# A two-layer encoder trunk: GpSimd's wide elementwise work on VectorE, and 512-column products with tokens stationary

## The chip, the cores and the metric

One core of a Trainium2 chip. The time is device microseconds of one execution; three unprofiled runs of the kernel before were taken, and one more execution under the profiler.

## The reference

`x` is 256 tokens x 1024, f32. Each of two layers applies three sub-layers, every one as `x = x + weight * rmsnorm(f(rmsnorm(x, g_pre)), g_post)`: a SwiGLU FFN (weight 0.5), a token mixer (weight 1), and a second FFN (weight 0.5).

```python
def swiglu(x, w_gate, w_up, w_down):
    return (jax.nn.silu(x @ w_gate) * (x @ w_up)) @ w_down      # 1024 -> 2816 -> 1024

def token_mixing(h, w_in, ...):
    proj = h @ w_in                                             # q, k, v of groups A, B, C
    o_a = chunk_band_attention(qa, ka, va, rel_bias)            # 6 heads of 64
    o_b = diff_attention(qb, kb, vb, lam, subln_g, lambda_init) # 4 heads, ALiBi
    o_c = stick_breaking_attention(qc, kc, vc)                  # 6 heads
    return jnp.concatenate([o_a, o_b, o_c]) @ w_out

def stick_breaking_attention(q, k, v):                          # per block of queries
    z = q @ k * scale
    log_beta = log_sigmoid(z)
    log_one_minus = where(strict, log_sigmoid(-z), 0.0)
    suffix = cumsum(log_one_minus, reverse=True) - log_one_minus
    a = where(strict, exp(log_beta + suffix), 0.0)
    return a @ v
```

## The kernel before

The six sub-layers are numbered `i` = 0 to 5: FFN, mixer, FFN, FFN, mixer, FFN. `x` stays in SBUF (`xs`), two tiles `t` of 128 tokens. Every f32 operand of a wide product is split into a high part of type fp32r and the rest, and `mm3` (L378 to L381) issues three matmuls: high by high, high by low, low by high.

**Weights** come through one `Stream` (L100 to L161). SyncE loads a chunk of 512 KB into one of four `raw` buffers; ScalarE casts it to `whi` (L142), VectorE subtracts to get `wlo` (L143), each in two pieces. `stream.ahead(n)` cuts the next n pieces, `stream.done(n)` frees the buffers of n used chunks, of which there are nine. Where these calls stand in the program sets where the pieces stand in ScalarE's and VectorE's queues.

**A norm** between sub-layers (class `Norm`, L305 to L375) scales the sub-layer's result, adds it to `xs`, and makes the next sub-layer's input `xg`: ScalarE sums squares by halves of 512 columns, GpSimd multiplies the first half by the gain and VectorE the second (`half_pre`, L355 to L359), VectorE adds the mean (L291), GpSimd takes the power (L286), VectorE and ScalarE scale one half each (L365, L366). PE transposes `xg` (`pt`, L374), and `split_copy` makes `xT`, high and low.

**An FFN** does its first 512 hidden columns with tokens stationary (`tokens_out`, L383): groups of 256 columns, gate and up, two of each, for both t; then `ht = sg * pu` on VectorE (L507), PE transposes it (`pth`, L513). The other 2304 columns go with weights stationary (`cols_pair`, L402: for each weight tile one matmul of 512 columns with the high and low parts of `xT`, L411, and one of 256, L413). `down` (L421) has tokens stationary and 512 columns.

```python
        pairs = [[c, c + 1], [c + 2, c + 3], [c + 4, c + 5], [c + 6, c + 7]]
        def gate(p, t, between=None):
            pg = psum.tile([P, 256], F32, tag="rot", name=f"pg{i}_{p}_{t}")
            tokens_out(pg, pairs[2 * p], t, between)
```

**A mixer** computes the values with tokens stationary in three groups of 384, 384 and 256 columns (L611 to L633), then queries and keys tile by tile (`pp`, `qkT`), while the heads' work is put between those products by a table of slots (`PLAN`): each head is a generator, and each of its steps has a slot number. `make_alibi` (L588) fills 4 x 256 columns on GpSimd (L593), `make_bias` (L642) negates the 128x1536 relative bias on GpSimd (L643; slot 41.05). A pair of stick-breaking heads (`pair_c`, L649 to L718; three pairs) makes the scores `s_c`, softplus `e` on ScalarE and VectorE (L678 to L682), its high part on ScalarE and the rest `l1`, `l0` on GpSimd (L690, L691), the sums `u_c` on PE, `z_c` on VectorE (L703, L704), the exponential on ScalarE (L706) and the products `o_c` on PE (L745). The softplus of pairs 0 and 2 and the bias lie in one tile, `yb`.

```python
            nc.gpsimd.tensor_sub(l1, e[:, 512:], h1.bitcast(F32))
            nc.gpsimd.tensor_sub(l0, e[:, :512], h0.bitcast(F32))
```

The first FFN (i = 0) begins while nothing has arrived yet; a table `START` sets the order of its first pieces, some of them on GpSimd.

Of the kernel before, what the change touches and what calls it, by code (L numbers as in the profile page):

```python
# [9 lines left out]
F32 = mybir.dt.float32  # L10
# [6 lines left out]
P = 128  # L17
# [10 lines left out]
QC, KC, VC = 1920, 2304, 2688  # L28
YA, YB, YC = 0, 384, 640
EPS = 1e-6  # L30
NEG = -1e30
FAR = 1e30

CH = 1152
NRAW = 4
# [44 lines left out]
}  # L80
NSPLIT = 9

# [17 lines left out]
class Stream:  # L100
# [64 lines left out]
def trunk_kernel(  # L165
    ctx: ExitStack,
    tc: tile.TileContext,
    x, f1_pre, f1_gate, f1_up, f1_down, f1_post,
    m_pre, w_in, rel_map, lq1, lk1, lq2, lk2, sub_g, w_out, m_post,
    f2_pre, f2_gate, f2_up, f2_down, f2_post,  # L170
# [55 lines left out]
    def plan_ffn(gate, up, down, l):  # L226
        g = {}
        for key, ap, c0 in (("g", gate, 0), ("u", up, 0), ("g", gate, 1), ("u", up, 1)):
            for h in range(2):
                stream.add(rows(ap, l, 4 * h, 4 * h + 4, c0 * 256, c0 * 256 + 256), 4, 256)  # L230
# [7 lines left out]
    V_CUTS = ((0, 3), (3, 6), (6, 8))  # L238
    QK_TILES = (
# [6 lines left out]
    def plan_mix(l):  # L246
        for c in (VC, VA):
            for k0, k1 in V_CUTS:
                stream.add(rows(w_in, l, k0, k1, c, c + 384), k1 - k0, 384)
        for h in range(2):  # L250
            stream.add(rows(w_in, l, 4 * h, 4 * h + 4, VB, VB + 256), 4, 256)
# [53 lines left out]
    class Norm:  # L305
# [6 lines left out]
        def post(self, banks, weight, slack=lambda k: None, last=None):  # L312
# [15 lines left out]
            for h in range(2):  # L328
                nc.vector.scalar_tensor_tensor(xs[:, t, HALVES[h]], fg[:, HALVES[h]], r[:, 0:1],  # L329
                                               xs[:, t, HALVES[h]], ALU.mult, ALU.add)  # L330
                if last is None:
                    self.half_pre(h)
                else:
                    last(t, h)
# [19 lines left out]

        def half_pre(self, h):  # L355
            t, sl = self.t, HALVES[h]
            mean_square(xs[:, t, sl], self.ss, h, "pre" + self.nm)
            eng = nc.gpsimd if h == 0 else nc.vector
            eng.tensor_mul(self.xg[:, sl], xs[:, t, sl], pre_tiles[self.i][:, sl])  # L359

        def end_pre(self):
            self.r = rstd_of(halves_mean(self.ss, "pre" + self.nm), 1, "pre" + self.nm)

            xg = self.xg
            nc.vector.tensor_scalar(xg[:, :512], xg[:, :512], self.r[:, 0:1], None, ALU.mult)  # L365
            nc.scalar.activation(xg[:, 512:], xg[:, 512:], AF.Copy, scale=self.r[:, 0:1])  # L366
# [27 lines left out]
    def cols_out(ps, c, quarter=lambda q: None):  # L394
# [79 lines left out]
    def ffn(i, turn1):  # L474
# [18 lines left out]

        pairs = [[c, c + 1], [c + 2, c + 3], [c + 4, c + 5], [c + 6, c + 7]]

        def gate(p, t, between=None):
            pg = psum.tile([P, 256], F32, tag="rot", name=f"pg{i}_{p}_{t}")
            tokens_out(pg, pairs[2 * p], t, between)
            sg = work.tile([P, 512], F32, tag="ta", bufs=TA, name=f"sgt{i}_{p}_{t}")
            nc.scalar.activation(sg[:, :256], pg, AF.Silu)  # L500
            return sg

        def up(sg, p, t, between=None):
            pu = psum.tile([P, 256], F32, tag="rot", name=f"pu{i}_{p}_{t}")
            tokens_out(pu, pairs[2 * p + 1], t, between)
            h = work.tile([P, 512], F32, tag="tb", bufs=3, name=f"ht{i}_{p}_{t}")
            nc.vector.tensor_mul(h[:, :256], sg[:, :256], pu)  # L507
            return h

        def token_close(h, p, t):  # L510
            pt = psum.tile([P, 2, P], F32, tag="rot", name=f"pth{i}_{p}_{t}")
            for j in range(2):
                nc.tensor.transpose(pt[:, j, :], h[:, j * P : j * P + P], ident)  # L513
            ts = slice(t * P, t * P + P)
            split_copy(hT_hi(2 * p, 2)[:, :, ts], hT_lo(2 * p, 2)[:, :, ts], pt)

        sg00 = gate(0, 0, (lambda: start(1)) if i == 0 else None)
        if i == 0:
            start(2)
        h00 = up(sg00, 0, 0, (lambda: start(3)) if i == 0 else None)  # L520
        if i == 0:
            start(4)
        else:
            sg10 = gate(1, 0, turn1)
        sg01 = gate(0, 1)
        stream.done(2)
        if i == 0:
            stream.ahead(4)
        h01 = up(sg01, 0, 1)
        stream.done(2)  # L530
        stream.ahead(4)
        if i == 0:
            sg10 = gate(1, 0)
        sg11 = gate(1, 1)
        stream.done(2)
        stream.ahead(4)
        new_h()
        token_close(h00, 0, 0)
        h10 = up(sg10, 1, 0)
        token_close(h01, 0, 1)  # L540
        h11 = up(sg11, 1, 1)
        stream.done(2)
        stream.ahead(4)
        token_close(h10, 1, 0)
        load_pre(i + 1)
        if i % 3 == 0:
            load_lambda(i // 3)
        closing = [(h11, 1, 1)]
        for f in range(4, KF, 2):
# [31 lines left out]
    def mix(i, l, turn1):  # L581
# [27 lines left out]
        c = stream.used  # L609
        vgroups = [(YC, [c, c + 1, c + 2], 384, "acc"), (YA, [c + 3, c + 4, c + 5], 384, "acc"),  # L610
                   (YB, [c + 6, c + 7], 256, "rot")]  # L611

        def values(g, t, between=None):
            y0, chunks, n, tag = vgroups[g]
            pv = psum.tile([P, 512], F32, tag=tag, name=f"pv{l}_{g}_{t}")
            tokens_out(pv[:, :n], chunks, t, between)
            (nc.scalar.copy if g != 1 else nc.vector.tensor_copy)(v[:, t, y0 : y0 + n], pv[:, :n])

        values(0, 0)
        stream.ahead(2)  # L620
        values(1, 0, turn1)
        stream.ahead(2)
        nc.scalar.preload_act_table_set("natural_log_exp_and_others")
        values(0, 1)
        stream.done(3)
        stream.ahead(6)
        values(1, 1)
        stream.done(3)
        stream.ahead(6)
        values(2, 0)  # L630
        values(2, 1)
        stream.done(2)
        stream.ahead(6)  # L633
        qkT = act.tile([P, 16, SEQ], F32, tag="bigh1", name=f"qkT{l}")
# [14 lines left out]
        def pair_c(j):  # L649
# [104 lines left out]
        def head_b(h):  # L754
# [51 lines left out]
        def head_a(h):  # L806
# [164 lines left out]
```

## Time and profile before

| | |
|---|---|
| median of 3 runs | 1038.41 us (1036.89 to 1039.23) |
| the profiled execution: own time / span | 1042.82 us / 1041.1 us |
| PE (TensorE) busy | 1018.3 us, 98% |
| VectorE (DVE) busy | 676.4 us, 65% |
| ScalarE (ACT) busy | 588.8 us, 57% |
| GpSimd (POOL) busy | 89.0 us, 9% |
| TensorE's mean granted clock | 0.986 |
| DMA | 183.16 MB, mean 176 GB/s |

The span runs from the first to the last instruction of the profiled execution; its own time is measured as that of the unprofiled runs is. A granted clock of 1.0 is 2.4 GHz and 0.5 is 1.2 GHz. A matmul's row shows when it starts and a modelled end, so that neighbours overlap; the step from one start to the next is what a matmul takes of the engine.

### The profile page before, as it was taken

The numbers are of one execution on the slowest core, as the hardware profiler recorded it, in microseconds if no ns is written. First come the engines' busy times: TensorE is split into PE (matmuls) and PEld (weight loads), VectorE is DVE, ScalarE is ACT, GpSimd is POOL, SyncE is SP. The second block draws the span as 40 slices with busy tenths as digits, with TensorE's granted clock in tenths as the row PEclk, the third lists the DMA queues.
The fourth block names the chain that finished last, engine by engine and source line by source line (L and its number), as shares of the span: only waits on it lengthen the run. The fifth ranks groups of instructions, "written<-read, shape, count | busy, mean of one in ns | idle before, by whom it ended". The sixth has DMA issues, their size and how long they took to land. (4 is left out here: it accounts for less than half of the span.)

```text
span 1041.1 us, 16033 instructions
## 1 busy us (share of the span) xinstructions
PE 1018.3 (98%) x5940; PEld 888.6 (85%) x5940; DVE 676.4 (65%) x1313; ACT 588.8 (57%) x1265; POOL 89.0 (9%) x105
## 2 busy tenths in 40 slices
PE   8899999999999999999999999999999999999997
PEld 7788888898887988888899888888998789888886
DVE  4576774668666677665566876656776665877642
ACT  5465654567655556654446666545666655756531
POOL 3100000111311100000030000002123020000000
PEclk9999999999899999999999999999998999999999
DMA  8866566566244366656726766664933334865631
GB/s 270 219 204 200 184 211 208 145 203 192 82 122 122 117 210 220 197 189 219 215 73 208 244 195 195 222 198 121 261 107 103 117 97 143 261 190 186 222 120 40
DMA packets 151005, 183.16 MB, mean 176 GB/s; under 512 B 5744, under 2 KB 134896, under 8 KB 150928
## 3 DMA queue, kind: packets, MB, share of 16 engines
q1 hardware_dynamic: 148448, 174.08, 54.2%
q0 software_dynamic: 2192, 7.54, 2.7%
q8 instruction: 46, 0.75, 0.3%
q10 hardware_dynamic: 288, 0.52, 0.1%
q14 instruction: 31, 0.25, 0.1%
HBM read 181.08 MB, written 1.05 MB: 175 GB/s over the span
## 5 line engine op out<-in xcount | busy, mean ns | idle before, releaser
L143 DVE TENSOR_TENSOR wlo<-raw,whi 128x512 fp32r<-128x512 f32 (+1 forms) x625 | 403.2, 700 | 169.2 <-ACT whi L142 168.7
L142 ACT CAST whi<-raw 128x512 fp32r<-128x512 f32 x630 | 350.0, 617 | 120.5 <-PE acc L381 70.8
L411 PE MATMUL pg<-xT,whi 128*128 128x512 f32 x576 | 205.5, 398 | 0.0
L411 PE MATMUL pu<-xT,whi 128*128 128x512 f32 x576 | 203.2, 395 | 0.0
L413 PE MATMUL pg<-xT,wlo 128*128 128x256 f32 x576 | 162.2, 282 | 0.0
L413 PE MATMUL pu<-xT,wlo 128*128 128x256 f32 x576 | 161.5, 280 | 0.0
L379 PE MATMUL acc<-whi,hh 128*128 128x512 f32 x352 | 137.2, 390 | 0.0
L381 PE MATMUL acc<-whi,hl 128*128 128x512 f32 x352 | 137.0, 389 | 0.0
L380 PE MATMUL acc<-wlo,hh 128*128 128x512 f32 x352 | 137.0, 389 | 0.0
L411 PEld LDWEIGHTS pg<-xT,whi 128*128 128x128 f32 x576 | 108.7, 189 | 25.2
L411 PEld LDWEIGHTS pu<-xT,whi 128*128 128x128 f32 x576 | 108.0, 187 | 25.3
L413 PEld LDWEIGHTS pg<-xT,wlo 128*128 128x128 f32 x576 | 109.7, 190 | 0.0
L413 PEld LDWEIGHTS pu<-xT,wlo 128*128 128x128 f32 x576 | 108.8, 189 | 0.0
L379 PE MATMUL pp<-xT,whi 128*128 128x256 f32 x256 | 78.9, 308 | 0.0
L379 PEld LDWEIGHTS acc<-whi,hh 128*128 128x128 f32 x352 | 66.1, 188 | 13.7
L381 PEld LDWEIGHTS acc<-whi,hl 128*128 128x128 f32 x352 | 66.1, 188 | 13.7
L380 PEld LDWEIGHTS acc<-wlo,hh 128*128 128x128 f32 x352 | 66.1, 188 | 13.5
L380 PE MATMUL pp<-xT,whi 128*128 128x256 f32 x256 | 74.4, 291 | 0.0
L381 PE MATMUL pp<-xT,wlo 128*128 128x256 f32 x256 | 74.2, 290 | 0.0
L286 POOL TENSOR_TENSOR r_post<-v_post,mhalf 128x1 f32<-128x1 f32 x12 | 6.6, 552 | 779.5 <-DVE v_post L291 779.5
L379 PEld LDWEIGHTS pp<-xT,whi 128*128 128x128 f32 x256 | 51.0, 199 | 7.7 <-issue 7.2
L418 ACT COPY side_pu<-pu 128x256 f32<-128x256 f32 x72 | 26.1, 368 | 47.9 <-PE pu L413 47.9
(247 smaller groups left out, 1559.0 us busy)
## 6 DMA issues: line engine op xcount, KB each, us to landing
raw<-in_ffn_w_gate_dram SPq DMA_DIRECT2D x88, 512.0 KB, 4.8
raw<-in_ffn_w_up_dram SPq DMA_DIRECT2D x88, 512.0 KB, 4.7
raw<-in_ffn_w_down_dram SPq DMA_DIRECT2D x88, 512.0 KB, 4.4
raw<-in_w_in_dram SPq DMA_DIRECT2D x36, 512.0 KB, 5.6
raw<-in_w_out_dram SPq DMA_DIRECT2D x16, 512.0 KB, 3.5
raw<-in_w_in_dram SPq DMA_DIRECT2D x8, 576.0 KB, 4.5
gpost<-in_ffn_post_g_dram POOLq DMA_DIRECT2D x4, 512.0 KB, 4.6
raw<-in_w_in_dram SPq DMA_DIRECT2D x4, 384.0 KB, 3.5
```

What stands on the lines that cost most here:

```text
L142: self.nc.scalar.copy(self.hi[:, a:b], raw[:, a:b])
L143: (lo or self.nc.vector).tensor_sub(self.lo[:, a:b], raw[:, a:b], self.hi.bitcast(F32)[:, a:b])
L286: nc.gpsimd.tensor_tensor(r[:, :width], v, mhalf[:, :width], ALU.pow)
L379: nc.tensor.matmul(ps, lhsT=ah, rhs=bh, start=first, stop=False)
L380: nc.tensor.matmul(ps, lhsT=ah, rhs=bl, start=False, stop=False)
L381: nc.tensor.matmul(ps, lhsT=al, rhs=bh, start=False, stop=last)
L411: nc.tensor.matmul(ps.rearrange("p a t -> p (a t)"), lhsT=wh[:, k % 4, cs], rhs=xT[:, k].rearrange("p a t c -> p (a t c)"), start=k == 0, ...
L413: nc.tensor.matmul(ps[:, 1, :], lhsT=wl[:, k % 4, cs], rhs=xT[:, k, 0].rearrange("p t c -> p (t c)"), start=False, stop=k == KT - 1)
L418: nc.scalar.copy(side, ps[:, 1, :])
```

## The change

GpSimd's wide elementwise work goes to VectorE: the first half of `xg` in ten norms, the alibi and bias multiplications, and `l1`, `l0` of the six stick-breaking pairs. GpSimd keeps the powers, memsets, iota, its DMA issues, and its pieces of the start. In a norm, both multiplications now stand in `end_pre`, around the mean.

Products with tokens stationary take 512 columns, in chunks of two k-tiles x 512: the FFNs' token stage (i = 2, 3, 5) is gate and up of four chunks each, for both t; the values of a mixer are two groups of 512, from an array `w_val` in which the host puts the value columns of C, B and A side by side. The first FFN keeps its groups of 256. With `last=True` (t = 1) `tokens_out` frees each chunk as soon as it is used and cuts two pieces ahead. A split buffer has 1024 columns instead of 1152, and there are ten instead of nine. PE's program has 5235 rows where it had 5625: 384 matmuls fewer (3 x 96 and 2 x 48), each with its weight load.

```diff
-CH = 1152
+CH = 1024
-NSPLIT = 9
+NSPLIT = 10
...
     def plan_ffn(gate, up, down, l):
+        if not stream.src:
...
+        else:
+            for ap in (gate, up):
+                for q in range(4):
+                    stream.add(rows(ap, l, 2 * q, 2 * q + 2, 0, 512), 2, 512)
...
+        for g in range(2):
+            for q in range(4):
+                stream.add(rows(w_val, l, 2 * q, 2 * q + 2, 512 * g, 512 * g + 512), 2, 512)
...
                 if last is None:
-                    self.half_pre(h)
+                    mean_square(xs[:, t, HALVES[h]], self.ss, h, "pre" + self.nm)
...
         def end_pre(self):
-            self.r = rstd_of(halves_mean(self.ss, "pre" + self.nm), 1, "pre" + self.nm)
+            t, xg, g = self.t, self.xg, pre_tiles[self.i]
+            nc.vector.tensor_mul(xg[:, :512], xs[:, t, :512], g[:, :512])
+            v = halves_mean(self.ss, "pre" + self.nm)
+            nc.vector.tensor_mul(xg[:, 512:], xs[:, t, 512:], g[:, 512:])
+            self.r = rstd_of(v, 1, "pre" + self.nm)
...
-    def tokens_out(ps, chunks, t, between=None):
+    def tokens_out(ps, chunks, t, between=None, last=False):
...
                 k += 1
+            if last:
+                stream.done()
+                stream.ahead(2)
...
+            gates, ups = list(range(c, c + 4)), list(range(c + 4, c + 8))
+            h0 = up(gate(gates, 0), ups, 0, turn1)
+            new_h()
+            sg1 = gate(gates, 1, None, True)
+            token_close(h0, 0, 4, 0)
+            closing = [(up(sg1, ups, 1, None, True), 0, 4, 1)]
...
-                nc.gpsimd.tensor_scalar(out=alibi[:, h, :], in0=dneg, scalar1=slope, scalar2=None, op0=ALU.mult)
+                nc.vector.tensor_scalar(out=alibi[:, h, :], in0=dneg, scalar1=slope, scalar2=None, op0=ALU.mult)
...
+            pv = psum.tile([P, 512], F32, tag="acc", name=f"pv{l}_{g}_{t}")
+            tokens_out(pv, list(range(c + 4 * g, c + 4 * g + 4)), t, between, t == 1)
...
-            nc.gpsimd.tensor_scalar(out=biasA, in0=biasA, scalar1=-1.0, scalar2=None, op0=ALU.mult)
+            nc.vector.tensor_scalar(out=biasA, in0=biasA, scalar1=-1.0, scalar2=None, op0=ALU.mult)
...
-            nc.gpsimd.tensor_sub(l1, e[:, 512:], h1.bitcast(F32))
-            nc.gpsimd.tensor_sub(l0, e[:, :512], h0.bitcast(F32))
+            nc.vector.tensor_sub(l1, e[:, 512:], h1.bitcast(F32))
+            nc.vector.tensor_sub(l0, e[:, :512], h0.bitcast(F32))
```

Lines of the changed kernel are numbered a little differently (the weight subtraction is L144, the bias L642). VectorE's queue around the first stick-breaking pair of layer 0, first as it was (`z_c_0` is the pair's score tile, `o_b` is group B's output, `wlo` a weight piece):

```order
L682 SCALAR_TENSOR_TENSOR yb_2378<-z_c_0_2741,yb_2378 128x768
L785 TENSOR_SCALAR yb_2378<-o_b_2_2791,rib_2_2650 128x64 x2
L143 TENSOR_TENSOR wlo_2804<-raw_2576,whi_2803 128x512 x2
L785 TENSOR_SCALAR yb_2378<-o_b_1_2834,rib_1_2563 128x64 x2
L785 TENSOR_SCALAR yb_2378<-o_b_0_2782,rib_0_2556 128x64 x2
L143 TENSOR_TENSOR wlo_2856<-raw_2611,whi_2855 128x512 x2
L703 TENSOR_TENSOR z_c_0_2741<-z_c_0_2741,u_c_0_2889 128x256
L704 TENSOR_TENSOR z_c_0_2741<-z_c_0_2741,u_c_0_2892 128x512
```

And in the changed kernel, on through the second pair's softplus (L681):

```order
L681 SCALAR_TENSOR_TENSOR yb_2334<-z_c_0_2697,yb_2334 128x768
L784 TENSOR_SCALAR yb_2334<-o_b_2_2747,rib_2_2606 128x64 x2
L144 TENSOR_TENSOR wlo_2760<-raw_2532,whi_2759 128x512
L689 TENSOR_TENSOR hl_c_0_2774<-yb_2334,hl_c_0_2774 128x256
L690 TENSOR_TENSOR l_c_0_2773<-yb_2334,h_c_0_2772 128x512
L144 TENSOR_TENSOR wlo_2760<-raw_2532,whi_2759 128x512
L784 TENSOR_SCALAR yb_2334<-o_b_1_2790,rib_1_2519 128x64 x2
L784 TENSOR_SCALAR yb_2334<-o_b_0_2738,rib_0_2512 128x64 x2
L144 TENSOR_TENSOR wlo_2812<-raw_2567,whi_2811 128x512 x2
L702 TENSOR_TENSOR z_c_0_2697<-z_c_0_2697,u_c_0_2845 128x256
L703 TENSOR_TENSOR z_c_0_2697<-z_c_0_2697,u_c_0_2848 128x512
...
L681 SCALAR_TENSOR_TENSOR e_c_1_2857<-z_c_1_2856,e_c_1_2857 128x768
L642 TENSOR_SCALAR yb_2334<-yb_2334 128x1536
```

The two splits of pair 0 (L689, L690) now stand between two weight pieces ahead of z_c, and the bias negation (L642), which GpSimd had after those splits, stands behind the second pair's softplus.

VectorE's queue at the end of FFN 2's token stage as it was (`ht` the multiplication L507, `hl` the split of its transpose):

```order
L143 TENSOR_TENSOR wlo_3786<-raw_3581,whi_3785 128x512 x2
L303 TENSOR_TENSOR hl_2_3795<-pth_0_0_3797,hh_2_3793 128x2x128
L507 TENSOR_TENSOR ht_1_0_3827<-sgt_1_0_3678,pu_1_0_3802 128x256
L303 TENSOR_TENSOR hl_2_3795<-pth_0_1_3829,hh_2_3793 128x2x128
L507 TENSOR_TENSOR ht_1_1_3859<-sgt_1_1_3775,pu_1_1_3834 128x256
L143 TENSOR_TENSOR wlo_3862<-raw_3740,whi_3861 128x512 x2
L143 TENSOR_TENSOR wlo_3870<-raw_3748,whi_3869 128x512 x2
L303 TENSOR_TENSOR hl_2_3795<-pth_1_0_3877,hh_2_3793 128x2x128
```

And in the changed kernel:

```order
L309 TENSOR_TENSOR hl_2_3611<-pth_0_0_3672,hh_2_3609 128x4x128
L144 TENSOR_TENSOR wlo_3687<-raw_3626,whi_3686 128x512 x2
L144 TENSOR_TENSOR wlo_3701<-raw_3640,whi_3700 128x512 x2
L144 TENSOR_TENSOR wlo_3715<-raw_3654,whi_3714 128x512 x2
L144 TENSOR_TENSOR wlo_3729<-raw_3668,whi_3728 128x512 x2
L514 TENSOR_TENSOR ht_102_1_3736<-sgt_98_1_3670,pu_102_1_3679 128x512
L309 TENSOR_TENSOR hl_2_3611<-pth_0_1_3758,hh_2_3609 128x4x128
```

The pieces of four chunks now stand ahead of the last `ht`, where before they stood behind it.

## Rows read from the trace of the kernel before

**Rows 1.** The page, part 1: busy us (share of the span) of each engine, instructions.

```profile
PE 1018.3 (98%) x5940; PEld 888.6 (85%) x5940; DVE 676.4 (65%) x1313; ACT 588.8 (57%) x1265; POOL 89.0 (9%) x105
```

**Rows 2.** Waits of PE: engine, output, line, releaser: us in total, times, longest.

```profile
PE o_c L745 <- ACT yb L706: 4.2, 2, 2.1
PE pth L513 <- DVE ht L507: 3.9, 1, 3.9
...
PE pt L374 <- DVE xg L365: 1.4, 2, 0.7
...
PE s_b L750 <- ACT qkT L847: 0.6, 1, 0.6
PE pv L381 <- DVE xT L303: 0.6, 2, 0.3
```

**Rows 3.** Timeline, layer 0, first stick-breaking pair: start, us, engine, line, op, xcount [idle before].

```profile
268.92 4.64 DVE L143 TENSOR_TENSOR wlo<-raw,whi 128x512 fp32r<-128x512 f32 x2
...
269.36 4.53 POOL L643 TENSOR_SCALAR yb<-yb 128x1536 f32<-128x1536 f32 x1
...
273.48 0.41 DVE L703 TENSOR_TENSOR z_c<-z_c,u_c 128x256 f32<-128x256 f32 x1
...
274.58 0.84 ACT L706 ACTIVATE yb<-z_c 128x768 f32<-128x768 f32 x1 [5.07 <-DVE z_c L704]
...
275.47 0.98 PE L745 MATMUL o_c<-yb,v 128*64 128x256 f32 x4 [2.10 <-ACT yb L706]
```

**Rows 4.** Windows: us, busy time (instructions) of each engine, granted clock, DMA share, GB/s.

```profile
275.67:285.91 10.24, 10.24 (x42) 8.57 (x40) 5.55 (x13) 8.13 (x14) 2.41 (x2) 0.50 0.21 82
784.26:794.50 10.24, 10.24 (x43) 9.29 (x42) 5.62 (x12) 7.14 (x13) 2.42 (x2) 0.50 0.25 70
336.87:340.29 3.42, 2.70 (x16) 2.06 (x16) 1.39 (x5) 1.94 (x4) 0.54 (x1) 1.00 0.00 0
43.56:46.98 3.42, 3.42 (x13) 2.93 (x12) 2.73 (x5) 1.18 (x3) 0.00 (x0) 0.50 0.80 218
```

**Rows 5.** Timeline of PE: first and last of eleven matmuls, 256, then 512 columns.

```profile
20.92 0.28 PE L379 MATMUL pg<-whi,xT 128*128 128x256 f32 x1
...
22.12 0.28 PE L380 MATMUL pg<-wlo,xT 128*128 128x256 f32 x1
...
500.70 0.39 PE L379 MATMUL acc<-whi,hh 128*128 128x512 f32 x1
...
502.97 0.39 PE L380 MATMUL acc<-wlo,hh 128*128 128x512 f32 x1
```

**Rows 6.** Groups of VectorE by form: busy us, mean ns, idle before.

```profile
L359 DVE TENSOR_TENSOR xg<-xs,gpre 128x512 f32<-128x512 f32 x10 | 16.7, 1667 | 0.3
...
L365 DVE TENSOR_SCALAR xg<-xg,r_pre 128x512 f32<-128x512 f32 x10 | 5.0, 500 | 7.0 <-POOL r_pre L286 7.0
...
L704 DVE TENSOR_TENSOR z_c<-z_c,u_c 128x512 f32<-128x512 f32 x6 | 4.1, 680 | 0.6 <-PE u_c L701 0.6
```

**Rows 7.** Timeline of the first FFN, token stage's close.

```profile
38.84 1.14 ACT L142 CAST whi<-raw 128x512 fp32r<-128x512 f32 x2 [2.95 <-DMA raw<-in_ffn_w_up_dram]
...
39.49 2.73 DVE L143 TENSOR_TENSOR wlo<-raw,whi 128x512 fp32r<-128x512 f32 x4 [3.35 <-ACT whi L142]
...
42.48 0.41 DVE L507 TENSOR_TENSOR ht<-sgt,pu 128x256 f32<-128x256 f32 x1
```

**Rows 8.** Timeline, layer 0, second stick-breaking pair.

```profile
288.58 0.28 PE L694 MATMUL u_c<-hl_c,tri 128*128 128x256 f32 x1
...
290.58 0.85 ACT L706 ACTIVATE e_c<-z_c 128x768 f32<-128x768 f32 x1 [1.00 <-DVE z_c L704]
...
294.55 0.66 PE L745 MATMUL o_c<-e_c,v 128*64 128x256 f32 x4
```

**Rows 9.** Windows of PE, line 411: eleven product pairs, then ten.

```profile
609.75:613.56 3.81, 3.81 (x12) 1.00 0.49 155
876.67:880.21 3.54, 3.54 (x12) 1.00 0.78 249
```

More of the change, by code (lines that the diff above doesn't have):

```diff
@@ L28 @@
 QC, KC, VC = 1920, 2304, 2688
-YA, YB, YC = 0, 384, 640
+VYC, VYB, VYA = 0, 384, 640
 EPS = 1e-6
@@ L154, in get @@
     def get(self, i):
+        while i not in self.parts:
+            at = self.cut, self.piece
+            self.ahead(1)
+            assert at != (self.cut, self.piece), "no buffer for a chunk that is needed"
         return self.parts[i]
@@ L168, in trunk_kernel @@
     x, f1_pre, f1_gate, f1_up, f1_down, f1_post,
-    m_pre, w_in, rel_map, lq1, lk1, lq2, lk2, sub_g, w_out, m_post,
+    m_pre, w_in, w_val, rel_map, lq1, lk1, lq2, lk2, sub_g, w_out, m_post,
     f2_pre, f2_gate, f2_up, f2_down, f2_post,
@@ L226, in plan_ffn @@
     def plan_ffn(gate, up, down, l):
[L227 to L230, printed above, removed]
+        if not stream.src:
+            for ap, c0 in ((gate, 0), (up, 0), (gate, 256), (up, 256)):
+                for h in range(2):
+                    stream.add(rows(ap, l, 4 * h, 4 * h + 4, c0, c0 + 256), 4, 256)
+        else:
+            for ap in (gate, up):
+                for q in range(4):
+                    stream.add(rows(ap, l, 2 * q, 2 * q + 2, 0, 512), 2, 512)
         for f in range(4, KF, 2):
@@ L236, in plan_ffn @@
             stream.add(rows(down, l, k, k + 1, 0, D), 1, D)
-    V_CUTS = ((0, 3), (3, 6), (6, 8))
     QK_TILES = (
@@ L246, in plan_mix @@
     def plan_mix(l):
[L247 to L251, printed above, removed]
+        for g in range(2):
+            for q in range(4):
+                stream.add(rows(w_val, l, 2 * q, 2 * q + 2, 512 * g, 512 * g + 512), 2, 512)
         for c in QK_TILES:
@@ L492, in hT_lo @@
             return tiles(hl, 14, k, n)
[L494 to L500, printed above, removed]
-            return sg
[L503 to L507, printed above, removed]
-            return h
@@ L510, in token_close, with gate @@
-        def token_close(h, p, t):
-            pt = psum.tile([P, 2, P], F32, tag="rot", name=f"pth{i}_{p}_{t}")
-            for j in range(2):
+        def gate(chunks, t, between=None, last=False):
+            n = stream.src[c][2]
+            pg = psum.tile([P, 512], F32, tag="rot", name=f"pg{i}_{chunks[0]}_{t}")[:, :n]
+            tokens_out(pg, chunks, t, between, last)
+            sg = work.tile([P, 512], F32, tag="ta", bufs=TA, name=f"sgt{i}_{chunks[0]}_{t}")[:, :n]
+            nc.scalar.activation(sg, pg, AF.Silu)
+            return sg
@@ new lines, in up, with token_close @@
+        def up(sg, chunks, t, between=None, last=False):
+            n = stream.src[c][2]
+            pu = psum.tile([P, 512], F32, tag="rot", name=f"pu{i}_{chunks[0]}_{t}")[:, :n]
+            tokens_out(pu, chunks, t, between, last)
+            h = work.tile([P, 512], F32, tag="tb", bufs=3, name=f"ht{i}_{chunks[0]}_{t}")[:, :n]
+            nc.vector.tensor_mul(h, sg, pu)
+            return h
+        def token_close(h, k, n, t):
+            pt = psum.tile([P, 4, P], F32, tag="rot", name=f"pth{i}_{k}_{t}")[:, :n, :]
+            for j in range(n):
@@ L513, in token_close @@
                 nc.tensor.transpose(pt[:, j, :], h[:, j * P : j * P + P], ident)
             ts = slice(t * P, t * P + P)
-            split_copy(hT_hi(2 * p, 2)[:, :, ts], hT_lo(2 * p, 2)[:, :, ts], pt)
-        sg00 = gate(0, 0, (lambda: start(1)) if i == 0 else None)
+            split_copy(hT_hi(k, n)[:, :, ts], hT_lo(k, n)[:, :, ts], pt)
         if i == 0:
+            pairs = [[c, c + 1], [c + 2, c + 3], [c + 4, c + 5], [c + 6, c + 7]]
+            sg00 = gate(pairs[0], 0, lambda: start(1))
@@ L519, in ffn @@
             start(2)
-        h00 = up(sg00, 0, 0, (lambda: start(3)) if i == 0 else None)
-        if i == 0:
+            h00 = up(sg00, pairs[1], 0, lambda: start(3))
             start(4)
-        else:
[L524 to L544, printed above, removed]
+            sg01 = gate(pairs[0], 1)
+            stream.done(2)
+            stream.ahead(4)
+            h01 = up(sg01, pairs[1], 1)
+            stream.done(2)
+            stream.ahead(4)
+            sg10 = gate(pairs[2], 0)
@@ new lines, in ffn @@
+            sg11 = gate(pairs[2], 1)
+            stream.done(2)
+            stream.ahead(4)
+            new_h()
+            token_close(h00, 0, 2, 0)
+            h10 = up(sg10, pairs[3], 0)
+            token_close(h01, 0, 2, 1)
+            h11 = up(sg11, pairs[3], 1)
+            stream.done(2)
+            stream.ahead(4)
+            token_close(h10, 2, 2, 0)
+            closing = [(h11, 2, 2, 1)]
+        else:
+            gates, ups = list(range(c, c + 4)), list(range(c + 4, c + 8))
+            h0 = up(gate(gates, 0), ups, 0, turn1)
+            new_h()
+            sg1 = gate(gates, 1, None, True)
+            token_close(h0, 0, 4, 0)
+            closing = [(up(sg1, ups, 1, None, True), 0, 4, 1)]
@@ L547, in ffn @@
             load_lambda(i // 3)
-        closing = [(h11, 1, 1)]
         for f in range(4, KF, 2):
@@ L609, in mix @@
         c = stream.used
-        vgroups = [(YC, [c, c + 1, c + 2], 384, "acc"), (YA, [c + 3, c + 4, c + 5], 384, "acc"),
-                   (YB, [c + 6, c + 7], 256, "rot")]
         def values(g, t, between=None):
[L614 to L617, printed above, removed]
+            pv = psum.tile([P, 512], F32, tag="acc", name=f"pv{l}_{g}_{t}")
+            tokens_out(pv, list(range(c + 4 * g, c + 4 * g + 4)), t, between, t == 1)
+            (nc.vector.tensor_copy if g else nc.scalar.copy)(v[:, t, 512 * g : 512 * g + 512], pv)
         values(0, 0)
@@ L621, in mix @@
         values(1, 0, turn1)
-        stream.ahead(2)
         nc.scalar.preload_act_table_set("natural_log_exp_and_others")
         values(0, 1)
-        stream.done(3)
-        stream.ahead(6)
         values(1, 1)
[L628 to L633, printed above, removed]
+        stream.ahead(4)
         qkT = act.tile([P, 16, SEQ], F32, tag="bigh1", name=f"qkT{l}")
@@ L710, in pair_c @@
             for h in range(2):
-                vs = slice(YC + 64 * (2 * j + h), YC + 64 * (2 * j + h) + 64)
+                vs = slice(VYC + 64 * (2 * j + h), VYC + 64 * (2 * j + h) + 64)
                 columns_out(o, h, v[:, :, vs], e0[:, h, :], e1[:, h, :])
@@ L773, in head_b @@
             yield
-            vs = slice(YB + 64 * h, YB + 64 * h + 64)
+            vs = slice(VYB + 64 * h, VYB + 64 * h + 64)
             pT = turned(f"b{l}_{h}", p0)
@@ L824, in head_a @@
                 pair_out[h // 2] = psum.tile([P, SEQ], F32, tag="rot", name=f"o_{nm}")
-            vs = slice(YA + 64 * h, YA + 64 * h + 64)
+            vs = slice(VYA + 64 * h, VYA + 64 * h + 64)
             columns_out(pair_out[h // 2], h % 2, v[:, :, vs], w[:, 0:2, :], w[:, 2, :])
@@ L938 @@
     "x", "ffn1_pre_g", "ffn1_w_gate", "ffn1_w_up", "ffn1_w_down", "ffn1_post_g",
-    "mix_pre_g", "w_in", "rel_map", "diff_lambda_q1", "diff_lambda_k1", "diff_lambda_q2",
+    "mix_pre_g", "w_in", "w_val", "rel_map", "diff_lambda_q1", "diff_lambda_k1", "diff_lambda_q2",
     "diff_lambda_k2", "diff_subln_g", "w_out", "mix_post_g",
@@ L956 @@
     dist = _np.clip(P + _np.arange(P)[:, None] - _np.arange(SEQ)[None, :], -CLIP, CLIP) + CLIP
-    inputs = dict(inputs, rel_map=rb[:, :, dist].transpose(0, 2, 1, 3))
+    w_in = _np.asarray(inputs["w_in"])
+    w_val = _np.concatenate([w_in[:, :, VC : VC + 384], w_in[:, :, VB : VB + 256], w_in[:, :, VA : VA + 384]], axis=2)
+    inputs = dict(inputs, rel_map=rb[:, :, dist].transpose(0, 2, 1, 3), w_val=w_val)
     arrays, args = {}, []
```

6 lines of the change are left out of this document (removed).

## The prediction, made blind

> **What bounds the kernel now.** I read the page's busy times first. TensorE (PE) is busy 98% of the span and GpSimd (POOL) 9% [rows 1], so taking work off GpSimd is worth nothing by itself: only PE's own work and PE's waits count. The list of PE's waits comes next [rows 2]. The reader is to see that few are left: two of 2.1 us before the output products of a stick-breaking pair (o_c), one in the first FFN, some tenths elsewhere.
>
> The timeline of the first pair in layer 0 shows where the 2.1 us is from [rows 3]. GpSimd's negation of the 128x1536 bias table runs from 269.36 for 4.53 us. Two weight pieces on VectorE (DVE) start at 268.92 and take 4.64 us together, where such subtractions of 512 columns take 0.68 each [rows 6], so 1.4. The subtraction z_c stands behind them, starts at 273.48, the exponential follows at 274.58, and o_c starts at 275.47 after 2.10 us of waiting. The other wait of this name is layer 1's.
>
> The windows show what follows [rows 4]: in the 10.24 us from 275.67, and from 784.26 in layer 1, the granted clock is 0.50, the lower of its two levels (1.2 GHz), though PE is busy throughout. Before that it had stood for most of a 2.1 us wait. In the third window PE was also short of work (2.70 of 3.42 us) and kept 1.00. In the fourth, behind the first FFN's wait of 3.9 us [rows 2], it had 0.50 for 3.42 us. So a stall costs its own length and then, if it is long enough, half of the time at the lower level.
>
> **The change part by part.** Measured against the profiled execution, 1042.8 us (span 1041.1); the median of the runs shown, 1038.4, is 4.4 lower.
>
> *Longer products.* With tokens stationary and 256 columns, a step from one matmul to the next is 120 ns: ten steps in 22.12 - 20.92 = 1.20 us [rows 5]. With 512 columns it is 227 ns: ten in 2.27 us. So doubling the columns saves 13 ns per matmul dropped. An FFN's token stage goes from 192 x 120 = 23.04 us to 96 x 227 = 21.77, -1.27; three FFNs change (i = 2, 3, 5), -3.8. The values have 96 matmuls of 384 columns (halfway, 173 ns) and 48 of 256, 22.40 us, and get 96 x 227 = 21.77: -0.63 per layer. Together **-5.1**. This work is on the path, since PE is never without the next matmul there.
> The Trainium skill (TensorE: Matmul & The Clock Gate, the section "Wait — 56ns, not 53.3ns?") states that a step at the full clock is the columns over 2.4 GHz and about 2.5 ns. By that, 384 fewer matmuls would be worth 384 x 2.5 = 1.0 us, an estimate from the page. The rows above disagree, 120 where that rule has about 109, and the rows decide here.
>
> *The bias negation on VectorE.* The 4.53 us on GpSimd become at most three times a VectorE multiplication by a scalar of 512 columns, 0.50 each [rows 6]: 1.5 us, and the order puts it behind the second pair's softplus (L681), no longer ahead of the first pair's z_c. What was doubled on VectorE falls back from 4.64 to 1.4, 3.3 us less. The two splits l1 and l0 are now VectorE's too, 0.68 and at most 0.68 (its 256 columns are half of that row's), ahead of the same z_c. So z_c comes at least 3.3 - 1.4 = 1.9 us earlier, and up to 2.9 where the splits fill time in which VectorE waited for a cast anyway; PE wanted o_c 2.1 earlier. I take both waits as gone, **-4.2**; at the low end 0.2 each stays.
>
> *The clock.* If the waits go, nothing ahead of the two low windows differs from other stretches of that stage, which have the full clock. Work that took 10.24 us at half speed takes 5.12: **-10.2** for both. Bounds: nothing, if another stall takes over, and 10.2.
>
> *The norm.* Two multiplications of 512 columns that ran at the same time, 1.67 us on VectorE [rows 6], become two in a row on VectorE, 2 x 0.68 = 1.36, with the mean between them, so that GpSimd's power and the second multiplication overlap. From the mixer to the FFN PE waits 0.7 us for the scaled rows, twice [rows 2]. Bounds: 0.3 to 0.7 each; I take 0.5, since the mean also waits for ScalarE's second square sum: **-1.0**. The other norms lie behind PE work that covers them (they show no wait), and cost nothing.
>
> *Values.* PE waits 0.3 us for the second half of xT in each layer [rows 2]; with 512 columns the products on the first half last longer by 12 x (227 - 173) = 0.6: **-0.6**. The alibi multiplications, eight of 256 columns at 0.50 or less, are 2 us per layer on VectorE at the stage's start; there VectorE has idle time, I cost them at nothing, and if that cover goes, they delay weight pieces by up to 2 us. The 0.6 us of s_b [rows 2] I leave as it is.
>
> *New waits.* In the FFNs with the new path the pieces of the next four chunks are issued ahead of the multiplication ht of the last token group. ht must end before PE's closing transposes. The first FFN has such an order today: VectorE's pieces from 39.49 for 2.73 us, behind a cast that waited 2.95 us for a transfer, and ht only at 42.48 [rows 7]; that wait costs 3.9 [rows 2]. Its cause is the start's crowded transfers, here they run steadily. If the pieces find their data, the eight casts and subtractions end about when PE wants ht: 0 to 1 us per FFN, taken as 0.4 x 3 = 1.2. In the second stick-breaking pair PE has 5.97 us from u_c at 288.58 to o_c at 294.55, and its exponential began at 290.58 [rows 8], so it was done 3.1 us early; at the full clock PE arrives there up to 2.1 + 5.1 = 7.2 us earlier; VectorE's chain starts earlier too, but is not itself faster, and the negation and two splits stand in it. I count 0.4 per layer, bounds 0 and 1.5. **+2.0** in all.
>
> Sum: -5.1 - 4.2 - 10.2 - 1.0 - 0.6 + 2.0 = **-19.1**. From the profiled execution that is 1023.7, from the median 1019.3. Part of the 4.4 between them may be time that the low clock cost this execution alone, which the unprofiled runs have less of to win back; I take **1020**.
> One term neither part of the change touches: products with weights stationary advance 346 ns per pair in one FFN (3.81 us for 11) and 354 in another (3.54 for 10) [rows 9]. Which step a stage falls into seems set by its start, and the starts move. With 288 pairs per FFN it is 2.2 us each way, for up to three FFNs; the likeliest case has 1012 to 1027 as its own range.
>
> **The rivals.**
> *A stall moves to the second pair.* For it: PE arrives earlier at the full clock, with a margin I make nearly zero. Against: the exponential was 3 us early and VectorE loses its 4.64 us. A wait of 1.5 us in each layer, and 1.7 (as in the first FFN) to 5.1 us of low clock behind it, gives back 6.4 to 13.2: 1026 to 1033, about **1030**.
> *Slower: the FFN closes.* ht stands behind four chunks' pieces in FFN 2, 3 and 5. If their transfers land some 4 us late, PE stands as in the first FFN: 3.9 us and 1.7 to 5.1 of clock, 5.6 to 9.0 each, 17 to 27 for three. It decides from about 7 us each: below, the other gains pay for it, above, the kernel is slower, up to **1047**. For it: the first FFN's wait. Against: VectorE's load there came from the start; in the later FFNs before, the same stage shows no wait.
> *The longer products return little.* If the 13 ns is not a cost of each matmul but is set by the weight loads of these stages, then 5.1 becomes 1.0 or less, and the result is **1024**. For it, the rule of the page cited above; against, rows 5, where both lengths run beside weight loads.
>
> **How the numbers follow.** Forecast 0.70, second pair 0.20, FFN closes 0.05, short return 0.05. The smallest difference that a measurement of this kernel can tell from none is about 0.2%, 2.1 us. Only the second rival, in its upper half, reaches no change or slower; with something for what I don't see: faster 0.95, same 0.02, slower 0.03. The range goes from 1011 (1019.3 less the 2.0 of new waits and the faster step of rows 9 in two or three FFNs) to 1031, which takes in most of the first rival.
>
> **What would show it.** Right: o_c is gone from PE's waits, PE's clock is 1.00 in both mixers, z_c of the first pair starts some 2 us earlier against the PE instruction that wants it, the token stages of FFN 2, 3 and 5 last 1.3 us less, PE's wait for the scaled rows (pt, from the mixer to the FFN) is 0.2 or less. Wrong: 0.50 in a window behind a pth or a second o_c wait; a step other than 227 ns in the 512-column stages; a wait of PE for weight pieces (wlo, whi), which are behind the added VectorE work.

## The result, and the profile after

The changed kernel takes 1034.3 us (median of 15 executions, 1030.8 to 1037.1), the kernel before beside it 1039.3 (1034.4 to 1047.2): ratio 0.9938, 95% interval 0.9918 to 0.9957. That is 5.0 us less by the medians and 6.4 by the ratio. Forecast were 1020 and a range from 1011 to 1031. The direction was right, at least two thirds of the gain is missing.

The profiled execution took 1034.26 us, 8.6 less than the one shown of before. The page's part 1 of the changed kernel, against [rows 1]:

```profile
PE 1005.8 (97%) x5556; PEld 860.2 (83%) x5556; DVE 672.9 (65%) x1333; ACT 586.6 (57%) x1249; POOL 43.2 (4%) x73
```

PE has 5556 matmuls where it had 5940, the 384 fewer on which the prediction counts (the numbers of program rows named ahead, 5625 and 5235, differ by 390). VectorE, which took over GpSimd's wide work, is busy 3.5 us less than before. PE's waits, against [rows 2] (us in total, times, longest):

```profile
PE pth L520 <- DVE ht L514: 10.9, 4, 2.7
...
PE s_b L749 <- ACT qkT L846: 2.3, 2, 1.7
...
PE pt L377 <- DVE xg L368: 1.0, 2, 0.5
```

The waits for o_c and pv are gone; pth, the transposes that close a token stage, has taken their place, with four waits instead of one (the first FFN's, and 2.74 us in each of FFN 2, 3 and 5). To see where the time went I took, in each trace, the start of each stage's first matmul, and the differences:

| stage (us) | before | changed | difference |
|---|---|---|---|
| up to the first FFN's weights-stationary stage | 43.14 | 44.57 | +1.4 |
| token stages, FFN 2 / 3 / 5 | 24.75 / 24.75 / 24.74 | 23.16 / 23.16 / 23.18 | -4.7 |
| weights stationary, FFN 2 / 3 / 5 | 102.02 / 100.20 / 102.02 | 105.11 / 104.81 / 104.84 | **+10.5** |
| values, layer 0 / 1 | 24.25 / 24.26 | 22.67 / 22.67 | -3.2 |
| queries, keys and heads, layer 0 / 1 | 78.64 / 77.96 | 72.75 / 71.71 | **-12.1** |
| output product and the norm behind it | 32.05 / 32.05 | 31.83 / 31.82 | -0.5 |

These make up the 8.6. The +1.4 of the first row lies in the start: the granted clock is 0.50 there for 6.83 us (10.52 to 17.35) in the changed kernel's profile and for 3.41 us (12.84 to 16.26) in that of before, worth up to 1.7 us by an estimate; a second profile of before, shown below, has 10.24 us of it (8.83 to 19.07), so this difference is not put down to the change. The mixers gained what was hoped; the three FFNs gave 10.5 back, right behind their token stages. The timeline of that place in FFN 2 (start, us, engine, line, operation, xcount, and the idle time before with its releaser):

```profile
351.56 0.60 PE L520 MATMUL pth<-ident,ht 128*128 128x128 f32 x4
351.76 0.60 ACT L506 ACTIVATE sgt<-pg 128x512 f32<-128x512 f32 x1 [2.04 <-PE pg L384]
...
355.90 0.39 PE L384 MATMUL pu<-spare,xT 128*128 128x512 f32 x1
...
356.32 0.59 ACT L308 CAST hh<-pth 128x512 fp32r<-128x512 f32 x1 [3.97 <-PE pu L384]
356.81 4.26 ACT L143 CAST whi<-raw 128x512 fp32r<-128x512 f32 x8
...
357.55 4.90 DVE L144 TENSOR_TENSOR wlo<-raw,whi 128x512 fp32r<-128x512 f32 x8
362.37 0.69 DVE L514 TENSOR_TENSOR ht<-sgt,pu 128x512 f32<-128x512 f32 x1
...
363.20 0.63 PE L520 MATMUL pth<-ident,ht 128*128 128x128 f32 x4 [2.74 <-DVE ht L514]
```

PE transposes the first token half at 351.56, but ScalarE's copy `hh` of it starts only at 356.32, 4.0 us after the silu, released by a PE product. The products up to 355.90 read `spare`: two weight chunks lie in that tile, which `hh` takes next (it has the same tag). So the copy waits for the last such product, in front of eight casts in ScalarE's queue; the eight subtractions follow them on VectorE, and `ht` stands behind those. The eight casts run without a gap: they wait for no transfer. In FFN 3, where the chunks lie in the two tiles `hh` and `hl` of the FFN before it, and in FFN 5 the copy has the same 3.97 us of waiting (it starts at 545.35 and 860.30) and the eight casts the same 4.26 us behind it. This is a theory so far (**A**); the prediction's second rival had late transfers as the cause (**B**).

The clock in three windows of 3.41 us behind the three waits, and in the old place of layer 0 (columns as in [rows 4]):

```profile
363.59:367.00 3.41, 3.41 (x22) 2.99 (x20) 1.02 (x2) 1.18 (x3) 0.00 (x0) 1.00 0.90 308
553.24:556.65 3.41, 3.41 (x12) 2.88 (x11) 1.02 (x2) 0.51 (x2) 0.00 (x0) 0.50 0.72 248
867.27:870.68 3.41, 3.41 (x13) 3.02 (x14) 1.02 (x2) 0.86 (x2) 0.00 (x0) 0.50 0.95 316
275.67:285.91 10.24, 10.24 (x73) 9.14 (x72) 9.60 (x21) 8.22 (x16) 0.41 (x1) 1.00 0.36 103
```

Three waits of 2.74 us each were followed by 1.2 GHz twice and not the third time. The mixer has the full clock.

### The profile page after: what moved, and what is told of

It reads as the page before. It is cut to its first block, busy times and chain, and to the rows that moved or that the text cites. A ratio compares the mean times of both kernels' runs of the same rounds, so it can differ in the third digit from the quotient of the medians.

```text
span 1032.5 us, 15222 instructions
## 1 busy us (share of the span) xinstructions
PE 1005.8 (97%) x5556; PEld 860.2 (83%) x5556; DVE 672.9 (65%) x1333; ACT 586.6 (57%) x1249; POOL 43.2 (4%) x73
## 3 DMA queue, kind: packets, MB, share of 16 engines
HBM read 181.08 MB, written 1.05 MB: 176 GB/s over the span
## 4 chain that ended last, share of the span: by engine, by line
PE 85%; DMA 5%; ACT 4%; DVE 3%; issue 1%; SPq 0%; POOL 0%; DVEq 0%; POOLq 0%; ACTq 0%
PE pu L418 13%; PE pg L418 13%; PE acc L382 9%; PE acc L384 9%; PE acc L383 9%; PE pu L420 7%; PE pg L420 6%; DMA raw<-in_ffn_w_up_dram 3%; DMA raw<-in_w_in_dram 3%; PE pp L382 2%; DVE wlo L144 2%; ACT whi L143 2%; PE pp L383 2%; PE pp L384 2%; PE pg L384 1%; PE pg L382 1%
## 5 line engine op out<-in xcount | busy, mean ns | idle before, releaser
L144 DVE TENSOR_TENSOR wlo<-raw,whi 128x512 fp32r<-128x512 f32 x625 | 395.4, 688 | 151.6 <-ACT whi L143 150.2
L382 PE MATMUL pp<-xT,whi 128*128 128x256 f32 x256 | 76.2, 298 | 0.0
L383 PE MATMUL pp<-xT,whi 128*128 128x256 f32 x256 | 72.3, 282 | 0.0
L382 PEld LDWEIGHTS pp<-xT,whi 128*128 128x128 f32 x256 | 48.8, 190 | 7.4 <-issue 6.3
L426 DVE TENSOR_TENSOR h<-pu,side_pu 128x256 f32<-128x256 f32 x72 | 30.0, 422 | 31.1 <-ACT side_pu L425 31.1
```

The costliest lines, as they stand in the source:

```text
L144: (lo or self.nc.vector).tensor_sub(self.lo[:, a:b], raw[:, a:b], self.hi.bitcast(F32)[:, a:b])
L382: nc.tensor.matmul(ps, lhsT=ah, rhs=bh, start=first, stop=False)
L383: nc.tensor.matmul(ps, lhsT=ah, rhs=bl, start=False, stop=False)
L426: nc.vector.tensor_add(out[:, j, :], ps[:, 0, :], side)
```

## The experiments

**The pieces behind ht.** In FFN 2, 3 and 5 the last group's eight pieces are issued after its multiplication.

```diff
-            closing = [(up(sg1, ups, 1, None, True), 0, 4, 1)]
+            h1 = up(sg1, ups, 1)
+            stream.done(4)
+            stream.ahead(8)
+            closing = [(h1, 0, 4, 1)]
```

> The changed kernel, with the eight weight pieces that the last token group issues in FFN 2, 3 and 5 put behind the multiplication ht. Theory A (ScalarE's copy hh of the first token half waits for the products that read the spare weight buffers, the eight casts stand behind it, and ht stands behind their subtractions): PE's wait pth for ht goes from 2.7 us to under 0.5 in the three FFNs, the two low-clock windows of 3.4 us go, time 1034.3 - 8.1 - 3.4 = about 1023 (1021 to 1027). Theory B (the transfers land late): the same here, since ht no longer stands behind the pieces. New cost if the pieces, now later, are late for the next chunks: a wait of PE for whi or wlo, up to 2 us per FFN.

1020.2 us (1018.8 to 1021.7), ratio to before 0.9819 (0.9789 to 0.9849). The timeline at the same place:

```profile
354.82 0.59 ACT L308 CAST hh<-pth 128x512 fp32r<-128x512 f32 x1 [3.97 <-PE pu L384]
355.31 4.26 ACT L143 CAST whi<-raw 128x512 fp32r<-128x512 f32 x8
...
356.18 0.69 DVE L514 TENSOR_TENSOR ht<-sgt,pu 128x512 f32<-128x512 f32 x1
356.79 4.90 DVE L144 TENSOR_TENSOR wlo<-raw,whi 128x512 fp32r<-128x512 f32 x8
...
358.80 0.60 PE L520 MATMUL pth<-ident,ht 128*128 128x128 f32 x4
```

The copy still waits 3.97 us and the casts still come late, but `ht` is ahead of their subtractions, and the second pth has no wait. No wait of PE for a piece appears in the list, and both low stretches in FFN 3 and 5 are gone: the delayed pieces are early enough. So what was missing, 14 us between the two medians, hangs on whether `ht` stands ahead of those eight pieces or behind them. The time is 0.8 us below the range expected. This kernel is faster than the one before and the changed one; it doesn't tell the two theories apart.

**The close late.** The transposes and the copy of the first half go behind the last group; the pieces stay ahead of `ht`.

```diff
-            token_close(h0, 0, 4, 0)
-            closing = [(up(sg1, ups, 1, None, True), 0, 4, 1)]
+            h1 = up(sg1, ups, 1, None, True)
+            token_close(h0, 0, 4, 0)
+            closing = [(h1, 0, 4, 1)]
```

> The changed kernel, with the transposes and the split copy of the first token half put behind the last token group of each FFN 2, 3 and 5; the pieces stay ahead of ht. Theory A: the casts of the next chunks start some 4 us earlier (about 352.5 in FFN 2 instead of 356.8), the wait pth for ht falls from 2.7 to under 0.5 us, time about 1023 (1021 to 1027). Theory B (late transfers): the casts wait for DMA instead, the wait stays about 2.7 us in each, time 1033 to 1035.

1024.9 us (1021.6 to 1028.6), ratio 0.9868 (0.9836 to 0.9901): in theory A's range.

```profile
351.71 1.13 ACT L143 CAST whi<-raw 128x512 fp32r<-128x512 f32 x2
...
354.01 1.14 ACT L143 CAST whi<-raw 128x512 fp32r<-128x512 f32 x2 [1.16 <-DMA raw<-in_ffn_w_gate_dram]
...
355.71 1.15 ACT L143 CAST whi<-raw 128x512 fp32r<-128x512 f32 x2 [0.56 <-DMA raw<-in_ffn_w_up_dram]
...
357.19 1.14 ACT L143 CAST whi<-raw 128x512 fp32r<-128x512 f32 x2 [0.32 <-DMA raw<-in_ffn_w_up_dram]
...
358.23 0.58 ACT L308 CAST hh<-pth 128x512 fp32r<-128x512 f32 x1
...
359.05 0.68 DVE L514 TENSOR_TENSOR ht<-sgt,pu 128x512 f32<-128x512 f32 x1
...
359.88 0.63 PE L520 MATMUL pth<-ident,ht 128*128 128x128 f32 x4
```

The first casts start at 351.71, straight behind the silu, as A has it; with B the order of the copy would not have mattered. The closing pth follows `ht` with no wait in the list. But a part of B is in these rows: the casts now wait 1.2, 0.6 and 0.3 us for transfers, and `ht` (to 359.73) ends only 0.15 us before PE starts the transposes.

**No spare buffers.** Both assignments of `stream.spare` give an empty list; nothing else is changed.

> The changed kernel without the spare weight buffers (which lie in the tile that the FFN's hidden values take later); order of all else as in the changed kernel. Theory A: with no product reading that tile, the copy hh of the first token half follows the silu of its group at once (idle before it under 0.5 us instead of 4.0), the eight casts start some 4 us earlier, the wait pth for ht falls from 2.7 to under 0.5 us. Theory B (late transfers): the casts come no earlier, the wait stays about 2.7 us. In both, fewer chunks are ready when a stage begins, so PE may wait for pieces there, some us in all; the time itself tells little.

1045.8 us in its one execution. ScalarE in FFN 2, and PE's longest waits:

```profile
359.90 0.60 ACT L506 ACTIVATE sgt<-pg 128x512 f32<-128x512 f32 x1 [1.60 <-PE pg L384]
360.39 0.58 ACT L308 CAST hh<-pth 128x512 fp32r<-128x512 f32 x1
```

```profile
PE pth L520 <- DVE ht L514: 6.5, 2, 4.4
PE pu L382 <- ACT whi L143: 4.7, 4, 1.2
PE pv L382 <- ACT whi L143: 4.6, 4, 1.2
```

The copy follows the silu at once: its 4 us were the spare buffers'. The closing wait is gone in FFN 2 and 5 (4.4 is the first FFN's); in FFN 3 one of 2.06 us stays, where casts waited 1.05 and 0.73 us for transfers and the last pieces were late again. So A is shown, with a second condition under it: where the copy is out of the way, the transfers leave next to no margin. That the spare buffers are needed, the waits for whi in token stages and values show; the time says no more.

**One half of the change at a time.** The kernel before with the moves to VectorE alone (the parts of the diff on `half_pre`, `end_pre`, alibi, bias, `l1`, `l0`), and the changed kernel with exactly those back on GpSimd, so that only the products are longer.

> The kernel before, with only the moves from GpSimd to VectorE (norms, alibi, bias, splits); products as before. If this part alone carries the gain in the mixers: no wait for o_c, clock 1.00 through both, the query and key stage about 6 us shorter in each layer, the norms 0.2 us each, no new wait in the FFNs: 1039.3 - 12.5 = about 1027. Rival: the mixers need the new value products too (earlier start of their pieces), the o_c wait stays at 1 to 2 us: 1036 to 1040.

> The changed kernel, with all of the moved elementwise work back on GpSimd; only the 512-column products and their chunks remain. The token stages and the values are 1.6 us shorter each (5 x 1.6 = 8 us less), the waits for ht in FFN 2, 3 and 5 stay (2.7 us each and some low clock, 8 to 11 us more), the o_c waits of 2.1 and the 10.2 us of low clock come back: 1039 to 1043, so no gain by itself. Rival: the products alone are a gain of 5 us or more: under 1035.

The moves alone: 1030.2 us (1027.4 to 1033.3), ratio 0.9911 (0.9884 to 0.9938), no o_c in the list of waits, the queries-and-keys stage at 70.8 and 71.0 us. The waits went as expected and the rival is out, but the time is 3 us above the 1027 expected. The products alone: 1044.6 (1039.2 to 1046.9), ratio 1.0040 (1.0014 to 1.0065): slower, and 1.6 us above the range expected. Their two longest kinds of wait:

```profile
PE pth L523 <- DVE ht L517: 9.2, 4, 2.7
PE o_c L747 <- ACT yb L708: 4.2, 2, 2.1
```

In that kernel the token stages and values are as short as in the changed one (23.2 and 22.7 us), so the products gain their 8 us, and the closes take more than that back. The longer products with a repaired close and without the moves were not run.

**The bias alone.** The kernel before with one line changed.

```diff
-            nc.gpsimd.tensor_scalar(out=biasA, in0=biasA, scalar1=-1.0, scalar2=None, op0=ALU.mult)
+            nc.vector.tensor_scalar(out=biasA, in0=biasA, scalar1=-1.0, scalar2=None, op0=ALU.mult)
```

> The kernel before with only the bias negation on VectorE (two instructions); splits, alibi and norms stay on GpSimd. If the 4.5 us negation beside VectorE's weight pieces is the whole cause: the two pieces beside it take 1.3 instead of 4.6 us, no wait for o_c, no low clock in the mixers, query and key stage 6 to 7 us shorter in each layer, 1039.2 - 12 = 1027 (1025 to 1031). Rival (the splits on GpSimd also hold VectorE back, or are late themselves): a wait for o_c or u_c of 0.5 to 2 us stays, 1031 to 1037.

1031.3 us (1027.7 to 1036.2), ratio 0.9894 (0.9857 to 0.9930): as much as all the moves together, within the intervals. The place of [rows 3], and the negation's group by form (busy, mean ns):

```profile
268.26 1.82 POOL L691 TENSOR_TENSOR l_c<-yb,h_c 128x512 fp32r<-128x512 f32 x1
269.61 1.62 DVE L143 TENSOR_TENSOR wlo<-raw,whi 128x512 fp32r<-128x512 f32 x2
...
271.15 0.41 DVE L703 TENSOR_TENSOR z_c<-z_c,u_c 128x256 f32<-128x256 f32 x1
...
274.00 0.66 PE L745 MATMUL o_c<-yb,v 128*64 128x256 f32 x4
```

```profile
L643 DVE TENSOR_SCALAR yb<-yb 128x1536 f32<-128x1536 f32 x2 | 1.9, 954 | 0.0
```

The two pieces take 1.62 us instead of 4.64, though GpSimd still has the splits; o_c has no wait, and both mixers have the full clock. The time lies at the border between the range expected and the rival's; the waits decide, and the rival's are not there. The negation itself is 0.95 us on VectorE, where GpSimd took 4.53. For the other moves (norms, alibi, splits) these two kernels show no gain of their own.

**The kernel before, a second time.**

> The kernel before, unchanged, profiled a second time. If the two waits for o_c and the 10.24 us of low clock behind each are in every execution: the same two rows again, 1037 to 1043. Rival (the length of the low clock differs from execution to execution, and the profile of before had much of it): one of the two stretches is 3.4 or 6.8 us or missing, and the time is lower by half of what is missing.

1039.8 us. The same waits of 2.1 us, but not the same clock:

```profile
PE o_c L745 <- ACT yb L706: 4.2, 2, 2.1
```

```profile
278.80:289.04 10.24, 10.23 (x74) 9.03 (x74) 7.48 (x16) 10.11 (x19) 2.64 (x3) 1.00 0.40 127
780.24:790.48 10.24, 10.24 (x43) 8.65 (x40) 5.64 (x13) 8.08 (x14) 2.41 (x2) 0.50 0.21 83
```

Behind the first wait the clock stays at 2.4 GHz, behind the second it falls for 10.24 us. The stage of the first mixer is 73.4 us long here and was 78.6 in the profile shown ahead, that of the second 78.0 both times. So the low stretch behind the first wait is there in one execution and not in the next, and the execution on which the sum rests had both. The mean clock of the 17 executions of before that ran beside the first four kernels above goes from 0.983 to 0.996 (one such stretch lowers it by 0.005, an estimate) and their time from 1046 to 1035, mostly together. At 0.996 an execution has room for some 8 us of low clock in all, so for neither stretch.

**The two repairs again.**

> The kernel with the pieces behind ht, a second time, beside the one with the late close: 1018 to 1023, spread under 4 us, no wait for ht in FFN 2, 3 and 5. If the 4.7 us between the two medians of the first runs were chance, the two come out within 2 us of each other.

> The kernel with the late close, a second time. If transfers that land late still hold ht up in some executions (the casts there waited 0.3 to 1.2 us for DMA, and ht ended with no margin), it stays some us above the other, 1022 to 1029, and the profile may show a wait for ht of up to 2 us in one FFN. Rival (chance): 1018 to 1023.

1021.4 (1019.6 to 1024.5, ratio 0.9793, 0.9763 to 0.9823) and 1025.7 us (1022.6 to 1027.2, 0.9823, 0.9794 to 0.9851). The difference of 4.3 us is that of the first time (4.7), so I don't take it for chance. What it consists of stays open: each time the one profiled execution of the late close was its fastest, and no wait for `ht` in FFN 2, 3 or 5 is listed. In the four profiles the weights-stationary stages of these FFNs take 302.8 us both times with the pieces behind `ht`, 303.4 and 303.2 with the late close; more of the difference is in the first FFN's (101.3 and 100.2 against 103.6 and 103.5), which neither edit touches. That transfers hold `ht` up in other executions fits the rows, but was not seen.

## Why the prediction was right and wrong

**The step that failed: the new waits at the FFNs' closes**, "0 to 1 us per FFN, taken as 0.4 x 3 = 1.2", on the condition "if the pieces find their data". They did find their data. The stages grew by 10.5 us, by 2.74 of wait in each (8.2) and half of 3.41 twice (3.4). That is 1.1 too much; the one stage whose product step changed is FFN 5's (ten pairs in 3.47 us from 873.40, where [rows 9] has 3.54), which at 288 pairs gives back some 2 us. The change does not touch that step, and in FFN 2 it differs between the two profiles of before (102.02 and 100.20 us for the stage). I asked only what a piece waits for (its transfer), not what stands ahead of it in ScalarE's queue: the change also moves the copy of the first half up, ahead of the products that still read the tile it writes. Before, the first copy stood behind the last product that reads `spare` (those of a gate there), and had no wait:

```profile
361.57 0.37 ACT L302 CAST hh<-pth 128x256 fp32r<-128x256 f32 x1
```

VectorE's queue, which I had written out, shows none of this; ScalarE's together with the tile's tag does. The second rival saw the right place and end (a wait and low clock, 4.4 us in two of the FFNs, against its 5.6 to 9.0) and the wrong cause. Of the signs of being wrong, the one that came is the 0.50 in a window behind a pth.

**The clock, -10.2: right in kind, too large for the median.** Both low stretches are gone in the changed kernel, and the mixers' stages are 12.1 us shorter in the two profiles. But the second profile of before had one stretch, not two, and the median clock of the 17 executions (0.989, against 0.986 and 0.988 in the two profiles) does not speak for two, so against a typical execution the term is nearer to 5, an estimate. That fits my remark that the 4.4 us between profile and median might be low clock that the other executions lack, and I corrected the result by 0.7 for it.

**The o_c waits, -4.2: right**, and the cause too: the bias alone does it. Its negation on VectorE was bounded at 1.5 us and took 0.95. The 0.4 per layer counted for the second pair did not come; no wait for it is listed, so the first rival is out.

**The longer products, -5.1: right step, more gain.** The step in the new token stage is the 227 ns of [rows 5]:

```profile
349.74 0.39 PE L383 MATMUL pg<-wlo,xT 128*128 128x512 f32 x1
...
351.33 0.39 PE L384 MATMUL pg<-whi,xT 128*128 128x512 f32 x1
```

Seven steps in 1.59 us. A token stage lost 1.59 us instead of 1.27, the values 1.59 a layer instead of 0.63 and 0.3 for the wait. A part of the first is only moved: four transposes pth of the first half stand inside the stage where six stood, and its closing pth is of four where it was of two. The rest was not taken apart. The third rival, that long products return little, is out.

**The norm, -1.0: 0.5.** The wait (1.4 us of two, [rows 2]) is 1.0 now. The multiplications became quicker as said, but GpSimd's power, which I had beside the second of them at no cost, is slower there:

```profile
330.33 0.68 DVE L366 TENSOR_TENSOR xg<-xs,gpre 128x512 f32<-128x512 f32 x1
330.56 0.86 POOL L292 TENSOR_TENSOR r_pre<-v_pre,mhalf 128x1 f32<-128x1 f32 x1 [2.75 <-DVE v_pre L297]
331.45 0.72 ACT L369 ACTIVATE xg<-xg,r_pre 128x512 f32<-128x512 f32 x1 [1.29 <-POOL r_pre L292]
```

It takes 0.86 us, and 0.81 in the mean of 12, where it had 0.55 in the kernel before, with no multiplication beside it. The same operation `r_post`, whose neighbour on VectorE (`fg_post`) reads PSUM and one tile of SBUF, still has 0.55; the first line is of before, the others of the changed kernel:

```profile
L286 POOL TENSOR_TENSOR r_pre<-v_pre,mhalf 128x1 f32<-128x1 f32 x12 | 6.6, 548 | 11.3 <-DVE v_pre L291 11.3
...
L292 POOL TENSOR_TENSOR r_pre<-v_pre,mhalf 128x1 f32<-128x1 f32 x12 | 9.7, 810 | 32.3 <-DVE v_pre L297 32.3
L292 POOL TENSOR_TENSOR r_post<-v_post,mhalf 128x1 f32<-128x1 f32 x12 | 6.6, 554 | 786.5 <-DVE v_post L297 786.5
```

The Trainium skill (SBUF — State Buffer, the section "SBUF: two separate sides") has a VectorE operation with two SBUF inputs and a GpSimd operation that reads SBUF exclude each other, whichever comes second waiting until the first is done. The trace agrees here: the power starts at 330.56 beside the multiplication and ends 0.41 us behind it (331.42 against 331.01). [Rows 3] agree in part: the weight pieces are held for most of the negation, 4.64 us instead of 1.4, but their row ends at 273.56, 0.33 us ahead of the negation's (273.89), so a wait to its end is not what the rows show.

**s_b** (the scores of a head of group B), left at 0.6, became 2.3 in this profile, and 0.7 to 3.2 in the four profiles of the repaired kernels. What PE waits for there is a copy on ScalarE; why that comes later than before was not traced.

Put together on the median: products and values -7.9, o_c -4.2, clock about -5, norm -0.5, s_b about +1.7, closes +10.5: -5.4, and -5.0 (medians) or -6.4 (ratio) was measured. Some of these terms come from a single profile each, so the fit is in part luck. Without the closes' 10.5 the sum is about -16, and the repaired kernel had -19 and -21: 3 to 5 us of that are in none of these terms. So a kernel whose closes are free does take the 1020 forecast, but not by the forecast's sum alone.

## What to carry to other kernels

When an instruction moves up in a queue, ask of it, as of a wait, what its output overwrites and who still reads that: a tile that changes hands between stages makes a copy wait for the last reader, and everything behind it on that engine waits along. Write out the queues of all engines on the path from there to the wait, not only the one in which the new order is seen. And size a term that rests on the clock from more than one execution.

## What had not been expected of the hardware

The clock's answer to a stall differs between executions: the same 2.1 us wait at the same place was followed by 10.24 us at 1.2 GHz in one and by none in the next, and of three waits of 2.74 us in one execution, two were followed by 3.41 us of it and one was not. Elementwise work of one GpSimd instruction can cost VectorE more than it spares: 4.53 us on GpSimd lengthened two weight pieces from 1.6 to 4.6 us, and the same work took 0.95 on VectorE.
